# State space layer on one core: layout copies shared by ScalarE and VectorE, two TensorE visits a quarter, gate stores moved in program order

## Chip, core and metric

The kernel runs on one core of a Trainium2 chip. The metric is the device time of one execution in microseconds (us); lower is better. Three executions of the kernel before took 1206.77, 1207.72 and 1211.47 us; their median is 1207.72 us.

## What is computed

The program is one layer of a hybrid backbone: 256 latent tokens and 128 context tokens (384 rows of 2048 channels) go through a modulated norm and one combined input projection, then through two mixers, a bidirectional state space layer (S5) and an attention, whose gated results are projected, merged and projected out. The part that the change touches is the state space layer and the gates next to it:

```python
def _s5_bidir(u, lam_bar, b_bar, c_re, c_im, d, h0_f, h0_b):
    ug = uf.reshape(n, L, SSM_GROUPS, SSM_GROUP).astype(jnp.complex64)
    bu_f = jnp.einsum('blgi,gpi->blgp', ug, b_bar[0])
    bu_b = jnp.einsum('blgi,gpi->blgp', ug, b_bar[1])
    h_f = _lin_scan(bu_f, lam_bar[0], h0_f)
    h_b = jnp.flip(_lin_scan(jnp.flip(bu_b, axis=1), lam_bar[1], h0_b), axis=1)
    y = (einsum('blgp,gip->blgi', h_f, c[0]) + einsum('blgp,gip->blgi', h_b, c[1])).real
...
    ys = ys * jax.nn.sigmoid(ys @ w_glu + b_glu)
    ys = ys * jax.nn.silu(z_s)
    merged = jax.nn.sigmoid(g_s) * p_s + jax.nn.sigmoid(g_a) * p_a
```

There are 64 groups of 16 channels, each with a state of 64 complex numbers, scanned over time in both directions.

## The kernel before

**Big matmuls.** Every projection is done in float32 with each operand split in a high and a low part (`hi`, `lo`; `hh`, `hl` for activations), so a product takes three matmuls. A weight block `raw` of 512 KB is loaded on SP's queue; for each half of it ScalarE writes `hi` (line 70) and VectorE (GpSimd in the first stage) writes `lo` (line 71). One half block is a step: 12 matmuls in `mode_b` (lines 192 to 194) or 9 wider ones in `mode_a` (lines 203 to 205). Four buffers of `raw`, `hi` and `lo` are kept, and `hi` and `lo` are prepared two to three steps ahead.

**Background work.** Everything else is written as Python generators. After the 12 matmuls of a step, `Background.step` lets each generator emit up to its next `yield`; a negative number means "come back so many steps later", a positive one is charged to the step's budget. So the program order of every engine is fixed by steps, and each engine works through its own order and waits at semaphores.

**The state space layer** (`ssm_half`, run twice, for 32 groups each) is such a generator. It has an input phase, a scan and an output phase.

- Input phase: four quarters `e` of 8 groups. `tables` (VectorE, six operations) builds `E`, the input matrices over four time steps; `turn` transposes it on TensorE (line 436) and `turn2` copies the result to `W1` on ScalarE (line 443); `kern` multiplies `CT` by `E` (line 452) and `kern2` picks its blocks to `KS` on VectorE; `drive` multiplies `W1` by the inputs `U` (line 478), once for the real part (`ri` 0) and once for the imaginary part; `drive2` copies each result to `H`, the scan's layout, in four ScalarE copies of 64 partitions by 384 elements (line 489), which write with a stride of 64 elements. `kturn` and `kturn2` transpose `KS` into `Kc`.
- These matmuls use the pool of five PSUM banks `bk`, handed out in rotation. A quarter takes nine: two for `drive` of the imaginary part, one for `kturn`, two for `turn`, two for `kern`, two for `drive` of the real part. So `kern` gets the banks that `drive` of the imaginary part filled five banks earlier.
- TensorE is visited three times in a quarter, a step apart: (`drive` imaginary, `kturn`, `turn`), then (`kern`), then (`drive` real). What drains a visit is emitted one step after it.
- Scan: 64 turns of four small VectorE operations on `H`.
- Output phase: for `x` in 0 to 7, `states` copies the states from `H` into a matmul operand `x4a` or `x4b`, four strided ScalarE copies of 64 by 384 (lines 585, 586); `outs` does 24 small matmuls (lines 597, 600) one step later; `act_out` applies GELU (line 611); `store` writes to DRAM.

**Gates.** `gate_zs` and `gate_gs` (lines 859 to 874) finish eight tiles each of the gates `z_s` and `g_s` right after the first stage and write them to DRAM scratch (`zss`, `gss`, 192 KB a store) through GpSimd's queue, two steps later. They are read again in the second half of the program. They are started from line 925 on, ahead of the state space layer in the list of generators.

In the same stretch SP's queue carries the layer's own inputs (`ssm_read`: C, B, D and the relayout of `U` out of scratch, many rows of 64 to 384 bytes) between the loads of `raw`.

Of the kernel before, what the change touches and what calls it, by code (L numbers as in the profile page):

```python
# [9 lines left out]
AF = mybir.ActivationFunctionType  # L10
# [116 lines left out]
def hybrid(ctx, tc, a):  # L127
    nc = tc.nc
    V, S, PE, GP, SP = nc.vector, nc.scalar, nc.tensor, nc.gpsimd, nc.sync
# [13 lines left out]
    def bank():  # L143
        return psb.tile([128, 512], F32, name="bk")
# [9 lines left out]
    def stt(o, x, s, y, op0, op1):  # L154
        return V.scalar_tensor_tensor(o, x, s, y, op0=op0, op1=op1)
# [232 lines left out]
    def ssm_half(hf, sp, yss):  # L388
        g0 = 32 * hf
        with pool("sh", "right") as t, pool("shx", "right", bufs=1) as tx, pool("shw", "right", bufs=2) as tw:  # L390
# [41 lines left out]
            def turn(e):  # L432
                pb = [bank() for _ in range(2)]
                for ri in range(2):
                    for j in range(4):
                        PE.transpose(pb[ri][:, 128 * j:128 * j + 128],
                                     E[e][:, ri, 2 * j:2 * j + 2].rearrange("p g s i -> p (g s i)"), ident)
                return pb

            def turn2(e, pb):  # L440
                W1[e] = tx.tile([128, 2, 4, 128], F32, name="W")
                for ri in range(2):
                    S.activation(W1[e][:, ri].rearrange("p j q -> p (j q)"), pb[ri], AF.Copy)

            def kern(e):
                pk = [bank() for _ in range(2)]
                for ri in range(2):
                    for j in range(4):
                        for d in range(2):
                            ps_ = slice(64 * d, 64 * d + 64)  # L450
                            gl = slice(8 * e + 2 * j, 8 * e + 2 * j + 2)
                            PE.matmul(pk[d][32 * j:32 * j + 32, 0:128],
                                      CT[ps_, ri, gl].rearrange("p g i -> p (g i)"),
                                      E[e][ps_, ri, 2 * j:2 * j + 2].rearrange("p g s i -> p (g s i)"),
                                      start=ri == 0, stop=ri == 1)
                return pk

            def kern2(e, pk):
                KS[e] = tw.tile([128, 2, 64], F32, name="KS")
                for d in range(2):  # L460
                    ts(KS[e][:, d], pk[d][:, 64:128], sp["ev"][:, 1:2], OP.mult)
                    stt(KS[e][:, d], pk[d][:, 0:64], sp["ev"][:, 0:1], KS[e][:, d], OP.mult, OP.add)

            def kturn(e):
                p = bank()
                for d in range(2):
                    PE.transpose(p[:64, 128 * d:128 * d + 128], KS[e][:, d], ident)
                return p

            def kturn2(e, p):  # L470
                S.activation(Kc[:, :, e], p[:64, 0:256].rearrange("p (d c) -> p d c", d=2), AF.Copy)

            def drive(e, ri):
                pb = [bank() for _ in range(2)]
                for j in range(4):
                    for g2 in range(2):
                        rows = slice(64 * g2, 64 * g2 + 64)
                        PE.matmul(pb[g2][:, 96 * j:96 * j + 96], W1[e][rows, ri, j], U[rows, 4 * e + j],  # L478
                                  start=True, stop=True)
                return pb  # L480

            def drive2(e, ri, pb):
                for g2 in range(2):
                    o = Hs[:, :, 1:33, ri, 8 * e + g2:8 * e + 8:2].rearrange("p b k g -> p g b k")
                    i = pb[g2][:, :384].rearrange("p (g n) -> p g n", g=4)
                    for d in range(2):
                        x = slice(64 * d, 64 * d + 64)
                        i_ = (i[x, :, ::-1] if d else i[x]).rearrange("p g (b k) -> p g b k", b=3)
                        S.activation(o[x], i_, AF.Copy)  # L489

            def ctables():
                for e in range(4):
# [18 lines left out]
            hold = {}  # L511
            for e in range(5):
                while e < 4 and e not in E:
                    yield -1
                if e:
                    drive2(e - 1, 0, hold[0])
                    hold[1] = drive(e - 1, 1)
                    hold["k"] = kturn(e - 1)
                if e < 4:
                    hold["t"] = turn(e)  # L520
                yield -1
                if e:
                    drive2(e - 1, 1, hold[1])
                    kturn2(e - 1, hold["k"])
                if e == 4:
                    break
                turn2(e, hold["t"])
                hold["p"] = kern(e)
                yield -1
                kern2(e, hold["p"])  # L530
                hold[0] = drive(e, 0)
                yield -1

            D2 = t.tile([128, 16, 4, 16], F32, name="x4b")
# [44 lines left out]
            def states(x):  # L579
                HB[x] = t.tile([128, 2, 4, 96], F32, name="x4a" if x % 2 else "x4b")  # L580
                gl = slice(4 * x, 4 * x + 4)
                for ri in range(2):
                    o = HB[x][:, ri].rearrange("p g (b k) -> p g b k", b=3)
                    i = Hs[:, :, 0:32, ri, gl].rearrange("p b k g -> p g b k")
                    S.activation(o[0:64], i[0:64], AF.Copy)
                    S.activation(o[64:128], i[64:128, :, ::-1, ::-1], AF.Copy)

            def outs(x):
                e, h = divmod(x, 2)
# [33 lines left out]
            for x in range(11):  # L623
                while x < 8 and x // 2 not in CL:
                    yield -1
                if x >= 4 and x % 2 == 0:
                    store(x // 2 - 2)
                if 2 <= x < 10:
                    act_out(x - 2)
                if 1 <= x < 9:  # L630
                    outs(x - 1)
                if x < 8:
                    states(x)
                yield -1

    def ssm(sp):
        for hf in range(2):
            yield from ssm_half(hf, sp, yss)
        p = bank()
        fo = ssp.tile([64, 2, 128], F32, name="fo")  # L640
        for ri in range(2):
            PE.transpose(p[:64, 128 * ri:128 * ri + 128], sp["fin"][:, ri], ident)
        S.activation(fo.rearrange("p r c -> p (r c)"), p[:64, :256], AF.Copy)
        for ri, n in enumerate(("out_re", "out_im")):
            SP.dma_start(dram(a[n], 0, [[64, 64], [4096, 2], [1, 64]]), fo[:, ri].rearrange("p (d q) -> p d q", d=2))
        yield 0.1
# [212 lines left out]
    def gate_zs(k):  # L859
        yield -1  # L860
        t = stg.tile([128, TOK], F32, name="sg")
        S.activation(t, zacc[k], AF.Tanh, scale=0.5)
        yield -1
        stt(zacc[k], t, 1.0, zacc[k], OP.add, OP.mult)
        yield -2
        GP.dma_start(zss[k], zacc[k])
        yield 0.1

    def gate_gs(k):
        yield -1  # L870
        S.activation(gacc[k], gacc[k], AF.Tanh, scale=0.5)
        yield -2
        GP.dma_start(gss[k], gacc[k])
        yield 0.1

# [13 lines left out]
    i = 0  # L889
    for s, (k0, nk) in enumerate(slices):  # L890
# [4 lines left out]
        for n in range(2 * len(plan[s])):  # L895
# [12 lines left out]
            for c, pv in enumerate(mode_k(i, hb, uk, kr)):  # L908
                w, k = divmod((c0 % 4096) // 128 + 4 // uk * hb + c, 8)
                if w == 0:  # L910
                    o = ua[:, k].rearrange("p (t n) -> p t n", t=T)
                    pv = pv.rearrange("p (n t) -> p t n", t=T)
                else:
                    o = zacc[k] if w == 1 else gacc[k]
                if kr:
                    tt(o, pv, o, OP.add)
                elif c % 2:
                    V.tensor_copy(o, pv)
                else:
                    S.activation(o, pv, AF.Copy)  # L920
                if end:
                    if w == 0:
                        SP.dma_start(us[k], ua[:, k])
                    elif w == 1:
                        g_zs.append(bg.add(gate_zs(k), True))
                    else:
                        g_zs.append(bg.add(gate_gs(k), True))
# [552 lines left out]
```

## Time and profile before

| | |
|---|---|
| three executions | 1206.77, 1207.72, 1211.47 us |
| the profiled execution | 1211.18 us, span of its core 1209.4 us |
| mean granted clock of TensorE | 0.989 of full speed |
| busy share of the span | TensorE 96%, VectorE 65%, ScalarE 47%, GpSimd 15% |
| HBM | 178 GB/s over the span |

The span runs from the first to the last instruction. The state space layer takes from about 270 to 690 us: its first transposes (`turn`) start at 292.13 and 499.33 us, the scans run from 339.5 to 424 and up to 632 us, and the output phases start at 437.5 and 647.8 us, the second ending at 689 us. An engine that isn't TensorE matters there only where TensorE stands still for it.

### The profile page before, as it was taken

The numbers are of one execution on the slowest core, as the hardware profiler recorded it, in microseconds if no ns is written. First come the engines' busy times: TensorE is split into PE (matmuls) and PEld (weight loads), VectorE is DVE, ScalarE is ACT, GpSimd is POOL, SyncE is SP. The second block draws the span as 40 slices with busy tenths as digits, with TensorE's granted clock in tenths as the row PEclk, the third lists the DMA queues.
The fourth block names the chain that finished last, engine by engine and source line by source line (L and its number), as shares of the span: only waits on it lengthen the run. The fifth ranks groups of instructions, "written<-read, shape, count | busy, mean of one in ns | idle before, by whom it ended". The sixth has DMA issues, their size and how long they took to land.

```text
span 1209.4 us, 19648 instructions
## 1 busy us (share of the span) xinstructions
PE 1159.6 (96%) x7215; PEld 1019.6 (84%) x7215; DVE 784.9 (65%) x1896; ACT 571.3 (47%) x1042; POOL 176.8 (15%) x150
## 2 busy tenths in 40 slices
PE   4899999999999999999999899998999999999997
PEld 3799999998898887989999788876787899878886
DVE  4555555676379963648996434478678846687873
ACT  4343333344853379585337834456454433333332
POOL 2355555672000000000000001110100000000000
PEclk9999999999999999999999999999898999999999
DMA  9987777478255485425544264446454257786661
GB/s 294 327 278 235 248 257 252 120 203 247 78 130 165 146 154 139 142 83 127 170 155 130 77 185 135 130 115 213 149 164 127 88 182 249 258 296 218 215 234 71
DMA packets 216116, 217.38 MB, mean 180 GB/s; under 512 B 64617, under 2 KB 170689, under 8 KB 215636
## 3 DMA queue, kind: packets, MB, share of 16 engines
q1 hardware_dynamic: 213940, 212.73, 58.0%
q0 software_dynamic: 1184, 3.18, 0.9%
q8 instruction: 57, 0.93, 0.3%
q10 hardware_dynamic: 896, 0.21, 0.1%
q14 instruction: 39, 0.32, 0.1%
HBM read 197.90 MB, written 16.87 MB: 178 GB/s over the span
## 4 chain that ended last, share of the span: by engine, by line
PE 78%; ACT 8%; DVE 7%; DMA 3%; issue 3%; SPq 1%; POOL 0%; DVEq 0%; ACTq 0%; POOLq 0%
PE m L192 10%; PE m L194 9%; PE m L193 9%; PE m L203 8%; PE m L205 8%; PE m L204 8%; PE m L854 5%; PE m L856 5%; PE m L855 5%; PE bk L726 2%; DVE lo L71 2%; ACT H L489 1%; PE bk L478 1%; ACT hi L70 1%; PE bk L1025 1%
## 5 line engine op out<-in xcount | busy, mean ns | idle before, releaser
L70 ACT ACTIVATE hi<-raw 128x512 fp32r<-128x512 f32 x464 | 286.9, 629 | 336.4 <-PE m L193 114.1
L71 DVE TENSOR_TENSOR lo<-raw,hi 128x512 fp32r<-128x512 f32 x368 | 250.7, 687 | 220.1 <-ACT hi L70 211.1
L192 PE MATMUL m<-hh,hi 128*128 128x384 f32 x832 | 288.7, 347 | 13.5 <-ACT hi L70 5.0
L194 PE MATMUL m<-hh,lo 128*128 128x384 f32 x832 | 281.2, 338 | 0.2
L193 PE MATMUL m<-hl,hi 128*128 128x384 f32 x832 | 280.5, 337 | 0.0
L203 PE MATMUL m<-hi,hh 128*128 128x512 f32 x480 | 190.4, 397 | 0.0
L205 PE MATMUL m<-hi,hl 128*128 128x512 f32 x480 | 187.5, 391 | 0.0
L204 PE MATMUL m<-lo,hh 128*128 128x512 f32 x480 | 187.3, 390 | 0.0
L192 PEld LDWEIGHTS m<-hh,hi 128*128 128x128 f32 x832 | 157.8, 190 | 28.6 <-ACT hi L70 8.0
L194 PEld LDWEIGHTS m<-hh,lo 128*128 128x128 f32 x832 | 157.7, 190 | 1.4 <-DVE lo L71 1.4
L193 PEld LDWEIGHTS m<-hl,hi 128*128 128x128 f32 x832 | 158.0, 190 | 0.1
L71 POOL TENSOR_TENSOR lo<-raw,hi 128x512 fp32r<-128x512 f32 x96 | 124.8, 1310 | 108.1 <-ACT hi L70 103.8
L854 PE MATMUL m<-hh,hi 128*128 128x384 f32 x384 | 133.1, 346 | 4.6 <-ACT ua L920 1.4
L855 PE MATMUL m<-hl,hi 128*128 128x384 f32 x384 | 129.1, 336 | 0.3 <-POOL hl L147 0.3
L856 PE MATMUL m<-hh,lo 128*128 128x384 f32 x384 | 129.4, 337 | 0.0
L203 PEld LDWEIGHTS m<-hi,hh 128*128 128x128 f32 x480 | 90.4, 188 | 21.4 <-issue 1.4
L205 PEld LDWEIGHTS m<-hi,hl 128*128 128x128 f32 x480 | 90.4, 188 | 19.3
L204 PEld LDWEIGHTS m<-lo,hh 128*128 128x128 f32 x480 | 90.5, 189 | 18.1
L854 PEld LDWEIGHTS m<-hh,hi 128*128 128x128 f32 x384 | 72.6, 189 | 13.5 <-issue 6.2
L855 PEld LDWEIGHTS m<-hl,hi 128*128 128x128 f32 x384 | 72.7, 189 | 0.5 <-POOL hl L147 0.5
L856 PEld LDWEIGHTS m<-hh,lo 128*128 128x128 f32 x384 | 72.5, 189 | 0.0
L147 POOL TENSOR_TENSOR rm<-rn,mhalf 128x24 f32<-128x24 f32 x4 | 18.1, 4515 | 365.2 <-DVE rn L152 365.2
(265 smaller groups left out, 1286.8 us busy)
## 6 DMA issues: line engine op xcount, KB each, us to landing
raw<-in_w_in_dram SPq DMA_DIRECT2D x160, 512.0 KB, 3.8
wa<-in_w_ada_dram SPq DMA_DIRECT2D x32, 1024.0 KB, 7.5
gw<-in_w_ada_dram SPq DMA_DIRECT2D x32, 512.0 KB, 5.8
raw<-in_w_o_dram SPq DMA_DIRECT2D x32, 512.0 KB, 6.1
raw<-in_w_ssm_out_dram SPq DMA_DIRECT2D x16, 512.0 KB, 3.4
raw<-in_w_att_out_dram SPq DMA_DIRECT2D x16, 512.0 KB, 5.8
raw<-in_w_glu_dram SPq DMA_DIRECT2D x8, 512.0 KB, 4.6
tgs<-sg SPq DMA_DIRECT2D x16, 192.0 KB, 1.9
```

Source lines behind the costliest of these rows:

```text
L70: self.nc.scalar.activation(h, t, AF.Copy)
L71: (self.nc.gpsimd if self.low_on_pool else self.nc.vector).tensor_tensor(l, t, f(h), op=OP.subtract)
L192: PE.matmul(o, wh[:, kk, w], xh[q][:, j, :], start=first and hb == 0 and kk == 0, stop=False)
L193: PE.matmul(o, wh[:, kk, w], xl[q][:, j, :], start=False, stop=False)
L194: PE.matmul(o, wl[:, kk, w], xh[q][:, j, :], start=False, stop=last and hb == 1 and kk == 1)
L203: PE.matmul(ps[r], xh[q][:, j, tk], wh, start=first and hb == 0, stop=False)
L204: PE.matmul(ps[r], xh[q][:, j, tk], wl, start=False, stop=False)
L205: PE.matmul(ps[r], xl[q][:, j, tk], wh, start=False, stop=last and hb == 1)
L726: PE.matmul(pab[b][32 * (k % 4):32 * (k % 4) + 32, 0:128 * nk], ct[:, kt, :], wa[s, i][:, k, :], start=kt < 4, stop=kt >= 12)
L854: PE.matmul(o, wh[:, w], hh[q][:, j, :], start=kk == 0, stop=False)
L855: PE.matmul(o, wh[:, w], hl[q][:, j, :], start=False, stop=False)
L856: PE.matmul(o, wl[:, w], hh[q][:, j, :], start=False, stop=kk == nk - 1)
```

## The change

`drive2` gives the bank of the odd groups (`g2` 1) to VectorE and keeps the other on ScalarE. `states` gives the imaginary part (`ri` 1) to VectorE. In the input phase `kern` and `drive` of the real part are emitted together, two steps after `turn`, and their drains `kern2` and `drive2` in the same step, right behind them. The gate stores are emitted 8 + 3k (`z_s`) and 9 + 3k (`g_s`) steps after the gate is done instead of two.

```diff
@@ drive2
                         i_ = (i[x, :, ::-1] if d else i[x]).rearrange("p g (b k) -> p g b k", b=3)
-                        S.activation(o[x], i_, AF.Copy)
+                        if g2:
+                            V.tensor_copy(o[x], i_)
+                        else:
+                            S.activation(o[x], i_, AF.Copy)
@@ the loop over quarters
                 if e:
-                    drive2(e - 1, 0, hold[0])
                     hold[1] = drive(e - 1, 1)
                     hold["k"] = kturn(e - 1)
...
                 turn2(e, hold["t"])
+                yield -1
                 hold["p"] = kern(e)
-                yield -1
+                hold[0] = drive(e, 0)
                 kern2(e, hold["p"])
-                hold[0] = drive(e, 0)
+                drive2(e, 0, hold[0])
                 yield -1
@@ states
-                    S.activation(o[0:64], i[0:64], AF.Copy)
-                    S.activation(o[64:128], i[64:128, :, ::-1, ::-1], AF.Copy)
+                    if ri:
+                        V.tensor_copy(o[0:64], i[0:64])
+                        V.tensor_copy(o[64:128], i[64:128, :, ::-1, ::-1])
+                    else:
+                        S.activation(o[0:64], i[0:64], AF.Copy)
+                        S.activation(o[64:128], i[64:128, :, ::-1, ::-1], AF.Copy)
@@ gate_zs
         stt(zacc[k], t, 1.0, zacc[k], OP.add, OP.mult)
-        yield -2
+        yield -8 - 3 * k
         GP.dma_start(zss[k], zacc[k])
@@ gate_gs
         S.activation(gacc[k], gacc[k], AF.Tanh, scale=0.5)
-        yield -2
+        yield -9 - 3 * k
         GP.dma_start(gss[k], gacc[k])
```

TensorE in the second quarter of the first half, around `kern` (L452). Before:

```order
L193 MATMUL m<-hl_103,hi 128x384
L194 MATMUL m<-hh_99,lo 128x384
L452 MATMUL bk<-E,CT 32x128 x16
L192 MATMUL m<-hh_99,hi 128x384
L193 MATMUL m<-hl_103,hi 128x384
```

And with the change:

```order
L193 MATMUL m<-hl_103,hi 128x384
L194 MATMUL m<-hh_99,lo 128x384
L452 MATMUL bk<-E,CT 32x128 x16
L478 MATMUL bk<-U,W 128x96 x8
L192 MATMUL m<-hh_100,hi 128x384
```

`kern` moved 12 matmuls back, to where `drive` (L478) stood, and 24 matmuls now lie between `turn` and it. In the first quarter of the first half alone `turn` itself also moved, 12 matmuls ahead, because the gates' generators no longer use up the budget of that step.

VectorE in the second half's input phase, from the drain of `kern` (KS) on; `E` and `q` belong to the table of the next quarter. Before:

```order
L155 SCALAR_TENSOR_TENSOR KS<-bk,ev,KS 128x64
L147 TENSOR_TENSOR E<-E,q_5617 128x4x8x16
L147 TENSOR_TENSOR q_5731<-me,preB 128x512
L71 TENSOR_TENSOR lo<-raw,hi 128x512
L147 TENSOR_TENSOR E<-me,preB 128x4x8x16 x2
```

And with the change (`L490` is `drive2`'s copy):

```order
L155 SCALAR_TENSOR_TENSOR KS<-bk,ev,KS 128x64
L490 COPY H<-bk 64x4x3x32 x2
L147 TENSOR_TENSOR E<-E,q_5617 128x4x8x16
L147 TENSOR_TENSOR q_5735<-me,preB 128x512
L71 TENSOR_TENSOR lo<-raw,hi 128x512
L147 TENSOR_TENSOR E<-me,preB 128x4x8x16 x2
L71 TENSOR_TENSOR lo<-raw,hi 128x512
L490 COPY H<-bk 64x4x3x32 x2
```

The last operation of a table now stands behind two copies that wait for `drive`.

GpSimd's queue at the end of the first stage. Before, the first ten of the sixteen stores stand between the last `lo` operations:

```order
L866 DMA zss<-zs_123 128x384
L866 DMA zss<-zs_122 128x384
L71 TENSOR_TENSOR lo<-raw,hi 128x512
L866 DMA zss<-zs_125 128x384
L866 DMA zss<-zs_124 128x384
L71 TENSOR_TENSOR lo<-raw,hi 128x512
L866 DMA zss<-zs_127 128x384
L866 DMA zss<-zs_126 128x384
L71 TENSOR_TENSOR lo<-raw,hi 128x512
L873 DMA gss<-gs_131 128x384
L873 DMA gss<-gs_130 128x384
```

And with the change:

```order
L402 MEMSET DT 128x1024
L873 DMA zss<-zs_122 128x384
L873 DMA zss<-zs_123 128x384
L880 DMA gss<-gs_130 128x384
L880 DMA gss<-gs_131 128x384
L873 DMA zss<-zs_124 128x384
L873 DMA zss<-zs_125 128x384
L880 DMA gss<-gs_132 128x384
L880 DMA gss<-gs_133 128x384
L873 DMA zss<-zs_126 128x384
L873 DMA zss<-zs_127 128x384
L538 MEMSET x4b 128x1024
```

All stores now stand behind the last `lo`, ten of them in one row ahead of the clearing of `x4b` (`D2`, which waits for the last table to have read `B`) and the other six behind it. SP's queue is in the same order before and after.

## Rows read from the trace of the kernel before

**Rows 1.** The page, part 1: busy time, share of the span, instructions.

```profile
PE 1159.6 (96%) x7215; PEld 1019.6 (84%) x7215; DVE 784.9 (65%) x1896; ACT 571.3 (47%) x1042; POOL 176.8 (15%) x150
```

**Rows 2.** Stretches (us): length, busy us (count) of each engine, clock, DMA share, GB/s.

```profile
286.00:290.00 4.00, 1.74 (x5) 1.38 (x6) 1.73 (x3) 1.64 (x3) 0.00 (x0) 0.80 1.07 317
...
345.00:425.00 80.00, 80.00 (x382) 69.67 (x381) 76.94 (x293) 27.60 (x47) 0.00 (x0) 1.00 0.57 153
...
450.00:460.00 10.00, 7.24 (x55) 6.01 (x54) 2.76 (x5) 9.81 (x17) 0.00 (x0) 1.00 1.01 156
...
640.00:700.00 60.00, 56.50 (x413) 48.06 (x412) 28.60 (x54) 46.82 (x72) 0.00 (x0) 0.97 0.35 100
```

**Rows 3.** The timeline of TensorE: start us, us, operation, [idle before, releaser].

```profile
281.12 0.33 PE L192 MATMUL m<-hh,hi 128*128 128x384 f32 x1
...
283.20 0.33 PE L192 MATMUL m<-hh,hi 128*128 128x384 f32 x1
...
295.18 0.67 PE L452 MATMUL bk<-E,CT 64*32 64x128 f32 x32
295.78 0.44 PE L192 MATMUL m<-hh,hi 128*128 128x384 f32 x1
...
305.83 0.40 PE L452 MATMUL bk<-E,CT 64*32 64x128 f32 x2
...
307.45 0.45 PE L192 MATMUL m<-hh,hi 128*128 128x384 f32 x1
...
309.76 1.14 PE L478 MATMUL bk<-U,W 64*128 64x96 f32 x16
```

**Rows 4.** Who waited for whom, whole span: us in total, times, longest.

```profile
PEld bk L452 <- ACT H L489: 6.1, 7, 1.4
```

**Rows 5.** Groups of instructions: line, engine, operation, tiles, count, busy us, mean ns.

```profile
L71 DVE TENSOR_TENSOR lo<-raw,hi 128x512 fp32r<-128x512 f32 x368 | 250.7, 687 | 220.1 <-ACT hi L70 211.1
...
L489 ACT ACTIVATE H<-bk 64x384 f32<-64x384 f32 x64 | 54.1, 845 | 15.4 <-PE bk L478 14.5
...
L1068 DVE COPY PT<-bk 128x384 f32<-128x384 f32 x16 | 8.1, 549 | 0.0
...
L147 DVE TENSOR_TENSOR hl<-sg,hh 128x384 fp32r<-128x384 f32 x8 | 6.5, 850 | 2.2 <-ACT hh L1302 1.9
...
L155 DVE SCALAR_TENSOR_TENSOR KS<-bk,ev,KS 128x64 f32<-128x64 f32 x16 | 4.5, 284 | 0.6
```

**Rows 6.** The timeline of ScalarE in the first output phase, one period of `x`.

```profile
464.01 0.68 ACT L611 ACTIVATE yg<-bk 64x192 f32<-64x192 f32 x2 [0.18 <-PE bk L600]
...
468.94 0.66 ACT L611 ACTIVATE yg<-bk 64x192 f32<-64x192 f32 x2
```

**Rows 7.** The timeline of TensorE in the first output phase: a wait and two visits.

```profile
456.92 0.44 PE L192 MATMUL m<-hh,hi 128*128 128x384 f32 x1 [2.60 <-ACT sg L1199]
...
466.19 0.55 PE L597 MATMUL bk<-x4b,W 128*64 128x96 f32 x8
...
470.07 0.55 PE L597 MATMUL bk<-x4a,W 128*64 128x96 f32 x8
```

**Rows 8.** The chain that ended last, around 280 us: start us, us, what.

```profile
279.80 7.67 DMA raw<-in_w_in_dram
```

**Rows 9.** The timeline of TensorE and VectorE behind that load.

```profile
288.26 0.55 PE L192 MATMUL m<-hh,hi 128*128 128x384 f32 x1 [2.30 <-ACT hi L70]
...
289.57 0.69 DVE L147 TENSOR_TENSOR E<-E,q 128x512 f32<-128x512 f32 x1
...
292.13 1.03 PE L436 MATMUL bk<-ident,E 128*128 128x128 f32 x8
```

**Rows 10.** DMA queues from 264 to 288 us: packets, MB, share of 16 engines.

```profile
q0 software_dynamic: 1024, 3.15, 37.6%
```

**Rows 11.** The timeline of GpSimd: its last `lo`, and what follows its stores.

```profile
270.90 1.30 POOL L71 TENSOR_TENSOR lo<-raw,hi 128x512 fp32r<-128x512 f32 x1
...
314.23 0.95 POOL L535 MEMSET x4b<- 128x1024 f32 x1 [33.75 <-DVE q L147]
```

## The prediction, made before the changed kernel was run

> **What bounds the kernel now.** I first looked at the busy shares on the page: TensorE is busy for 1159.6 of 1209.4 us [rows 1], so only its 50 us of idle time, and what it does at a lower clock, can be won. Next I read the stretches [rows 2], to see in which of them it stands still: not in a scan (80.00 of 80 us busy, with VectorE at 76.94), but next to the scans, in the input and output phases and where the first of them begins. Third, the timeline of TensorE there [rows 3] and the waits [rows 4], to see whom it waits for: ScalarE's copies to and from `H` in both phases, and one weight load at 288 us.
>
> **Input phase.** A step of 12 matmuls takes 2.08 us unbroken (281.12 to 283.20) but 2.31 us from the end of one visit to the start of the next (307.45 to 309.76), so a visit costs 0.23 us beside its own matmuls [rows 3]. `kern` takes 0.60 us where it does not wait (295.18 to 295.78), and 1.62 us in the second quarter (305.83 to 307.45) [rows 3]: two of its matmuls go, then it waits for the bank that `drive2` is still emptying. Over the program its weight loads wait 6.1 us for those copies [rows 4]; six quarters have the wait, the first of each half has not.
>
> With the change `kern` stands two steps after `turn` and its banks' drain is two copies on each of two engines instead of four in a row on one. Two ScalarE copies of 0.845 us [rows 5] and `hi`, `Kc` and `W1` behind them are over well before 24 matmuls (4.2 us) are. So the 6.1 us go. The eight visits that fall away, one in each quarter, give 8 x 0.23 = 1.8 us. **Term B: -7.9 us.**
>
> What is late next is VectorE. Its new copy, 64 partitions by 384 elements from PSUM, written with a stride, is not in the trace. Below it lies a copy of 384 contiguous elements from PSUM, 0.549 us; above it an operation of 384 elements that reads with a long stride, 0.850 us [rows 5]. ScalarE takes 0.845 us for the same strided copy, so I take 0.85 and keep 0.55. In a quarter VectorE then has three `lo` and six table operations of the same size (9 x 0.69), four for `KS` (4 x 0.284) and four copies (4 x 0.85): 10.7 us [rows 5], if nothing overlaps. TensorE's quarter is 11.7 us now (three steps of 2.31, `kern` 1.62, the rest visits), and would be 10.4. The two are level, and only while a table is being built, beside three of a half's four quarters. The drains now wait at the head of VectorE's queue for TensorE to reach `drive`, and behind them stand the next table's last operation and `lo`. `lo` is two steps ahead, so 4.6 us of cover; the table's last operation ends 2 x 0.85 + 0.7 us = 2.4 us after `drive`, and `turn` wants it one step, `drive` and `kturn` later, some 3.6 us after. It fits with 1.2 us to spare, which a copy of 1.45 us would use up. I charge nothing for it.
>
> **Output phase.** One `x` takes ScalarE 4.93 us (464.01 to 468.94) [rows 6] and TensorE 3.88 us (466.19 to 470.07) [rows 7]. ScalarE falls back by 1 us with each `x` until the two steps of cover are gone; then TensorE waits: 2.60 us at 456.92 [rows 7], and 3.5 us between 640 and 700 us, where it is busy for 56.50 of 60 us [rows 2]. There the clock is at 0.97 on the mean [rows 2]: TensorE, after standing still, runs a part of the stretch at the lower (1.2 GHz) of its levels, and over 60 us that is worth 1.8 us. Two of the four copies gone, ScalarE needs 4.93 - 2 x 0.85 = 3.2 us an `x` and is faster than TensorE; VectorE needs 2 x 0.85 + 0.69 = 2.4 us, 3.8 with two table operations, just below 3.88. So the waits go: 2.6 + 3.5 + 1.8 = 7.9 us. I leave 0.4 for the first `x` of a half, where tables and copies meet. **Term C: -7.5 us.**
>
> The clock's 1.8 us hang on the idle time. But after 2.60 us of idle time ahead of 456.92 [rows 7] the clock of that stretch stayed at 1.00 [rows 2]. The Trainium skill, "TensorE: Matmul & The Clock Gate", section "What's actually happening", says that the slow clock is the default and that activity releases it; by this rule the 1.8 us come back with the waits. By the row at 456.92 alone the two are not tied, and the sum would be 1.8 us smaller.
>
> **The start of the first half.** A `raw` load issued at 279.80 lands 7.67 us later, at 287.5 [rows 8]. TensorE waits 2.30 us for it and then takes 3.87 us for 12 matmuls (288.26 to 292.13) [rows 9] instead of 2.31: 1.56 us, since the clock is at 0.80 there, partly at 1.2 GHz [rows 2]. That is 3.9 us to win. In this stretch the 16 engines are full (DMA share 1.07) [rows 2], and the gate stores on GpSimd's queue use 37.6% of 24 us, 9.0 us for 16 stores or 0.56 us each [rows 10]. But a later place in program order does not by itself hold a store back: GpSimd's last `lo` ends at 272.2 us [rows 11], and after it nothing but the clearing of `DT` stands ahead of ten of the stores, so these go one behind the other from some 273 us on, while the load is under way. Only the six behind the clearing of `x4b`, which waits until 314 us [rows 11], leave the crowded stretch. That moves 6 x 0.56 = 3.4 us of transfers away, so the load lands between 284.1 (all of it gained) and 287.5 us (nothing gained).
>
> Against it stands that `turn` of the first quarter has moved ahead of these 12 matmuls. It needs the last operation of the first table, which stands on VectorE behind the `lo` of this very load and ends at 290.26, 2.8 us after it landed [rows 8, 9]. TensorE would reach `turn` at 285.96 (288.26 less the wait) and stand until landing + 2.8: 0.9 us with a landing at 284.1, 4.3 us at 287.5. So the place changes by -3.0 us (0.9 for 2.3, and the clock back) to +2.0 us. I take the middle. **Term A: -0.5 us.** The moved drains, the six late stores and the swapped copies add no instruction to TensorE, and SP's queue keeps its order; the late stores meet DMA engines that are mostly idle.
>
> **Sum.** -7.9 - 7.5 - 0.5 = -15.9 us. The profiled execution took 1211.18 us, which gives 1195.3; it lies 3.5 us above the median of the three, 1207.72, from which I get 1191.8. I forecast 1192 us.
>
> **The rivals.**
>
> R1, the gates are not spread. Of the sixteen stores ten still leave together, right when the load is on its way; then it lands at 287.5 as before, and the early `turn` makes the place worse. For it speaks the order of GpSimd's queue; against it that none goes before 273 us any more. Term A is +2.0 instead of -0.5: 1194.5, say 1195 us. The Trainium skill, "DMA: Bandwidth & Descriptors", section "Queues, rings and completion order", says that each DMA engine takes turns between the queues that have work, packet by packet; by this rule the load's delay follows from what is outstanding beside it and not from what went before, which is this rival. No row here shows single packets.
>
> R2, VectorE takes ScalarE's place in the input phase: at 1.1 us or more a copy its quarter (9 x 0.69 + 4 x 0.284 + 4 x 1.1 = 11.7 us) is as long as today's, and only the merged visits of term B are left: 1192 + 6.1 = 1198 us. For it speaks that the two engines are level at 0.85 already; against it that the longest row of 384 elements is 0.85 us [rows 5] and that each half's last quarter has no table beside it.
>
> R3, what is won before a scan is lost in it: VectorE is busy for 76.94 of 80 us there [rows 2]. If it enters with a backlog of more than 3.1 us, TensorE waits for `lo` in the scan and term B is gone in both halves: 1192 + 7.9 = 1200 us. Against it: the last quarters have no tables, so the backlog has gone by then.
>
> R4, slower. The in-order wait: `lo` stands behind `kern2` and the two copies, which wait for `drive`. It decides once two copies, the table's last operation and `lo` (2 x copy + 2 x 0.69) take longer than the 4.6 us of cover, so from 1.6 us a copy. At 2.0 us VectorE's quarter is 9 x 0.69 + 4 x 0.284 + 4 x 2.0 = 15.3 us against 11.7 now. Over the six quarters with tables that is +22 us; the output phase (2 x 2.0 + 0.69 = 4.7 us an `x`, near ScalarE's 4.93 now) wins nothing: 1207.7 + 22 = 1230 us. Only the strided write speaks for it; the row of ScalarE's same write, 0.845 us [rows 5], speaks against.
>
> **How the numbers follow.** A measurement of this kernel can tell about 0.5%, 6 us, from no change. The forecast has 0.65, R1 0.13, R2 0.11, R3 0.08, R4 0.03. The forecast's own range is 1185 to 1197: below, all 3.9 us of the load and 0.55 us copies, and some 3 us in which the profiled execution may have stood still more than the median; above, the clock's 1.8 us not coming back and half a microsecond a quarter of late tables. R2 and R3 end at 1198 and 1200, so the range is 1184 to 1200. Faster by over 0.5% means below 1201.7: the forecast, R1, R2 and 0.02 of R3, which ends close to that bound, 0.91. The rest of R3 is within 0.5%: 0.06. Slower: 0.03.
>
> **What would show it.** Right: `kern` in 0.60 us with `drive` right behind it and no wait for `H`; VectorE's copies at 0.55 to 0.85 us; ScalarE below 85% in the output phases, TensorE without the waits at their ends; ten stores in one row from 273 us on, six behind the clearing of `x4b`. Wrong: copies above 1.1 us; TensorE idle before `turn` for more than 2 us at 286 (term A); new waits of TensorE for `lo` or for a table.

## The result and the profile after

The changed kernel takes **1192.12 us** (median of 4 runs, 1188.56 to 1198.52) where the kernel before takes 1209.3 us on the same chip. The ratio is **0.9852**, 95% interval 0.9825 to 0.988: faster by 1.2 to 1.75%. In a later set of runs the same kernel came to 0.9877 (0.9857 to 0.9898), so single sets differ by some 3 us. The forecast was 1192.0 us. Its sum held; of its three terms one, the output phase, was 4 us too small, beyond its interval. One of `split_only`'s eight executions took 2892.59 us and is left out of its ratio.

The page of the changed kernel, part 1: busy time, share of the span, instructions.

```profile
PE 1144.7 (96%) x7215; PEld 1011.2 (85%) x7215; DVE 834.2 (70%) x1960; ACT 519.6 (44%) x978; POOL 176.3 (15%) x150
```

Against [rows 1], 64 instructions and 52 us left ScalarE, and 49 us came to VectorE. TensorE keeps its 7215 matmuls and yet is busy for 15 us less. The stretches say why (length, busy us of each engine, clock, DMA share, GB/s), here of the changed kernel:

```profile
286.00:290.00 4.00, 2.77 (x17) 2.77 (x18) 3.93 (x7) 2.13 (x4) 0.00 (x0) 1.00 0.62 191
300.00:340.00 40.00, 40.00 (x392) 37.24 (x391) 33.29 (x65) 25.32 (x39) 4.09 (x7) 1.00 0.40 125
345.00:425.00 80.00, 80.00 (x375) 68.75 (x374) 76.76 (x280) 27.54 (x46) 0.00 (x0) 1.00 0.56 153
425.00:461.00 36.00, 36.00 (x278) 32.14 (x278) 26.63 (x44) 25.89 (x41) 0.00 (x0) 1.00 0.87 172
640.00:700.00 60.00, 60.00 (x423) 49.43 (x422) 31.99 (x60) 32.31 (x60) 0.00 (x0) 1.00 0.47 136
```

In 640 to 700 us TensorE was busy for 56.50 of 60 us at a clock of 0.97, and ScalarE for 46.82 [rows 2]; now TensorE has no gap, its clock is at 1.00 and ScalarE needs 32.31 (the output phase lies some 12 us earlier here; from 628 to 688 us TensorE has no gap either, and ScalarE is busy for 34.81). The scan (345 to 425) is as it was. The timeline of TensorE shows the rest (start us, us, operation, [idle before, releaser]); the changed kernel in the first half's input phase:

```profile
296.40 0.44 PE L192 MATMUL m<-hh,hi 128*128 128x384 f32 x1 [1.38 <-ACT sg L1202]
...
306.22 0.67 PE L452 MATMUL bk<-E,CT 64*32 64x128 f32 x32
306.82 1.14 PE L478 MATMUL bk<-U,W 64*128 64x96 f32 x16
```

`kern` goes through in 0.60 us with `drive` right behind it, in every quarter; the 6.1 us of [rows 4] are gone. But TensorE has a new wait at 296.40, which no step of the prediction had.

To compare stages without the shift between the traces, the table takes when single visits start, from the view of their lines: the first `turn` (L436), the last `drive` (L478) of the first half and so on. Lengths in us, from each event to the next; "out" is the product with `DT` in `outs`.

| from ... to | before | `gates_only` | `in_only` | `out_only` | after |
|---|---|---|---|---|---|
| start of the program ... first `turn` | 292.1 | 285.5 | 293.1 | 291.2 | 285.4 |
| ... last `drive`, first half | 45.7 | 51.5 | 41.3 | 45.7 | 46.6 |
| ... first out (the scan) | 105.9 | 105.9 | 105.9 | 106.0 | 105.9 |
| ... last out, first half | 35.7 | 37.1 | 37.3 | 32.2 | 32.2 |
| ... first `drive`, second half | 25.9 | 25.9 | 25.6 | 25.8 | 25.6 |
| ... last `drive`, second half | 39.1 | 39.1 | 36.9 | 39.1 | 36.9 |
| ... first out (the scan) | 109.6 | 109.3 | 109.3 | 109.4 | 109.3 |
| ... last out, second half | 34.5 | 34.7 | 34.6 | 29.9 | 29.9 |
| ... end | 520.9 | 518.3 | 518.0 | 518.3 | 515.0 |

The middle columns are the first experiments. The first two rows have to be taken together, since the spread gates pull the first `turn` 12 matmuls ahead. Ahead of every other event stand equally many big matmuls in all five. The last row has nothing of the change in it and still differs by up to 6 us; most of that is the clock. Stretches of the kernel before and of the changed kernel:

```profile
800.00:940.00 140.00, 129.61 (x722) 106.11 (x720) 111.61 (x294) 69.74 (x175) 10.75 (x3) 0.95 0.51 158
800.00:940.00 140.00, 129.01 (x770) 108.82 (x769) 112.47 (x299) 72.83 (x184) 6.29 (x2) 1.00 0.49 156
```

0.95 over 140 us is worth 7 us; the three columns between have 0.98. The traces of the two outer columns are of executions of 1211.18 us, 3.5 above the median before, and of 1188.56 us, 3.6 below the median after, so they lie further apart than the medians do.

### The profile page after: what moved, and what is told of

It is laid out like the page before. It is cut to its first block, busy times and chain, and to the rows that moved or that the text cites. A ratio compares the mean times of both kernels' runs of the same rounds, so it can differ in the third digit from the quotient of the medians.

```text
span 1186.8 us, 19637 instructions
## 1 busy us (share of the span) xinstructions
PE 1144.7 (96%) x7215; PEld 1011.2 (85%) x7215; DVE 834.2 (70%) x1960; ACT 519.6 (44%) x978; POOL 176.3 (15%) x150
## 4 chain that ended last, share of the span: by engine, by line
PE 87%; DVE 5%; ACT 3%; DMA 2%; issue 2%; SPq 1%; POOL 0%; ACTq 0%; DVEq 0%; POOLq 0%
PE m L192 11%; PE m L194 11%; PE m L193 11%; PE m L203 9%; PE m L204 9%; PE m L205 9%; PE m L861 6%; PE m L862 5%; PE m L863 5%; PE bk L733 2%; PE bk L478 1%; PE bk L604 1%; PE bk L607 1%; PE bk L1032 1%; DMA raw<-in_w_in_dram 1%
```

## The experiments

Changes in us below are the ratio's distance from 1 times the median of before in the same set (1211.06, 1210.09, 1209.62 us).

**Each part alone.** Three kernels are the one before with one part of the diff, and a fourth is the changed kernel without the spread gates (yields -2 again).

`gates_only`:

```diff
-        yield -2
+        yield -8 - 3 * k
         GP.dma_start(zss[k], zacc[k])
...
-        yield -2
+        yield -9 - 3 * k
         GP.dma_start(gss[k], gacc[k])
```

> The kernel before with the gate stores spread and nothing else. The theory (term A): the raw load of the first half is issued some 4 us earlier and lands at 284 instead of 287.5, but the turn visit is pulled ahead of its table and waits, so 0 to 4 us are won, about 2; the clock in 286 to 294 is 1.00 instead of about 0.8. Rival R1 (the queue shares bandwidth whatever the order of the stores): nothing, ratio 1.000 within 0.002, and the raw load still lands about 287.5.

> The changed kernel with the gate stores back at their old places. The theory: loses what the spread brought, 0 to 4 us against the changed kernel (ratio to before 0.985 to 0.989), and PE again runs at a low clock between 286 and 294. R1: same as the changed kernel, 0.985.

Measured: 0.9993 (0.9977 to 1.0009), -0.8 us, and `gates_back` 0.9858 (0.9839 to 0.9877), no different from the changed kernel. The spread gates are worth nothing that can be measured. The load that the prediction has landing at 287.5 shows it. ScalarE takes up its two halves when it has landed; in the changed kernel, and in the same kernel run again:

```profile
284.49 1.16 ACT L70 ACTIVATE hi<-raw 128x512 fp32r<-128x512 f32 x2 [6.72 <-DMA raw<-in_w_in_dram]
```

```profile
288.21 1.15 ACT L70 ACTIVATE hi<-raw 128x512 fp32r<-128x512 f32 x2 [7.63 <-DMA raw<-in_w_in_dram]
```

In the six traces without the spread it lies between 283.97 and 288.68 us, in the eight with it between 284.00 and 288.21: run against run differs more than kernel against kernel. The low clock was no sign either: 270 to 300 us have it at 0.94 in `gates_only` and `gates_back`, and at 1.00 in `in_only`, which has no spread.

`in_only` is the diff's `drive2` and its loop over quarters; `out_only` is its `states`.

> The kernel before with the input phase alone changed (copies of drive shared, two visits a quarter). The theory (term B): -7.9 us, ratio 0.9935, no wait of the kern visit for a copy to H. R2 (VectorE takes ScalarE's place): about -4, ratio 0.997, and waits of PE for VectorE in 300 to 340.

Measured: 0.9947 (0.9927 to 0.9966), -6.4 us (-8.8 to -4.1). In the table the first two rows, up to the first half's last `drive`, lose 3.4 us, and the second half's input phase (rows 5 and 6) 2.5.

> The kernel before with the states' imaginary parts copied by VectorE and nothing else. The theory (term C): -7.5 us, ratio 0.994, PE without gaps in 440 to 460 and in 640 to 700, clock 1.00 there. R3 (won time lost elsewhere): under 3 us, ratio 0.998 or above.

Measured: 0.9903 (0.9887 to 0.9919), -11.8 us (-13.7 to -9.8), clearly more than either theory. The table finds 4.6 us of it in the second half and 3.5 in the first against before's own trace, 4.9 to 5.1 in the first against `gates_only` and `in_only`, which have the same output phase as before. What differs is the clock. Before's trace keeps 1.00 after the 2.60 us wait [rows 7]; `in_only` has the same wait, then this (stretches as above, and the row of the wait ahead of them):

```profile
453.56 0.44 PE L192 MATMUL m<-hh,hi 128*128 128x384 f32 x1 [2.58 <-ACT sg L1202]
```

```profile
425.00:461.00 36.00, 33.26 (x223) 29.82 (x222) 19.98 (x32) 30.42 (x44) 0.00 (x0) 0.95 0.82 160
450.00:454.00 4.00, 1.42 (x8) 1.09 (x7) 0.00 (x0) 3.92 (x7) 0.00 (x0) 1.00 0.95 178
454.00:458.00 4.00, 4.00 (x16) 4.00 (x15) 3.42 (x6) 3.94 (x8) 0.00 (x0) 0.57 0.44 119
```

16 matmuls in 4 us at 0.57: most of it ran at 1.2 GHz, which cost (1 - 0.57) x 4 = 1.7 us. Of five traces with this wait three show the drop (`gates_only`, `in_only`, `order_only`; 0.95 in each over the phase) and two don't (before, `split_only`). With the change there is no wait and no drop. `out_only`, the same stretches:

```profile
425.00:461.00 36.00, 36.00 (x257) 32.30 (x256) 30.41 (x50) 23.61 (x38) 0.00 (x0) 1.00 0.87 177
640.00:700.00 60.00, 60.00 (x432) 50.73 (x431) 37.25 (x69) 35.35 (x61) 0.00 (x0) 1.00 0.41 115
```

The parts add up: -0.8 - 6.4 - 11.8 = -19.0 us, against -17.9 (0.9852) for all of them.

**The order or the sharing?** I had given `kern`'s vanished wait to both. `order_only` is before with the visits merged and every copy on ScalarE; `split_only` is before with `drive2`'s copies shared and the old order.

```diff
@@ order_only: the loop over quarters
                 if e:
-                    drive2(e - 1, 0, hold[0])
                     hold[1] = drive(e - 1, 1)
...
                 turn2(e, hold["t"])
+                yield -1
                 hold["p"] = kern(e)
-                yield -1
+                hold[0] = drive(e, 0)
                 kern2(e, hold["p"])
-                hold[0] = drive(e, 0)
+                drive2(e, 0, hold[0])
                 yield -1
@@ split_only: drive2
-                        S.activation(o[x], i_, AF.Copy)
+                        if g2:
+                            V.tensor_copy(o[x], i_)
+                        else:
+                            S.activation(o[x], i_, AF.Copy)
```

> The kernel before with the input phase's two visits a quarter and all copies left on ScalarE. Theory: it was the place of kern that removed its wait, so most of the input phase's gain comes from the order alone, -4 to -5 us (0.996), but ScalarE's four copies at the head of its queue (4 x 0.85 = 3.4 us) delay the evacuations of PSUM behind them by 1.7 us more than in the changed kernel, so each half keeps a wait of 2.5 to 3 us. Rival: the sharing of the copies is what counts, and the order alone brings nothing or loses (1.000 or above).

> The kernel before with drive2's copies shared and the visits in the old order. Theory: two copies in a row (1.7 to 2.1 us) instead of four (3.4 us) empty the bank before kern wants it, so the 6.1 us of kern's waits go without the order too; the drains stand a step later than in the changed kernel, so no PSUM evacuation is held up: -6 us (0.995), as good as both together. Rival: the order is needed, kern still waits 0.5 us or more in each of six quarters: -3 us or less (0.9975 or above).

Measured: `order_only` 0.9981 (0.9967 to 0.9996), -2.3 us; `split_only` 0.994 (0.9918 to 0.9962), -7.3 us, as good as both together. Either of the two takes `kern`'s wait away: in neither trace does it wait for a copy to `H` any more. `split_only` in the second quarter, `kern` in its old place (TensorE, start us, us):

```profile
306.90 0.67 PE L452 MATMUL bk<-E,CT 64*32 64x128 f32 x32
307.50 0.44 PE L192 MATMUL m<-hh,hi 128*128 128x384 f32 x1
```

But only the sharing brings the whole gain. With the order alone TensorE then waits for an evacuation behind ScalarE's four copies. The waits of TensorE in the second half's input phase, 484 to 546 us (waiting line, released by: us, times, longest), of `order_only`, and a stretch right behind this wait:

```profile
PE m L192 <- ACT sg L1199: 2.7, 1, 2.7
```

```profile
530.00:534.00 4.00, 4.00 (x25) 3.36 (x24) 1.22 (x2) 1.09 (x2) 0.00 (x0) 0.50 0.91 283
```

The wait costs the clock as well. The granted clocks on record say the same of all executions: 0.9885 on the mean of 10 of `order_only`, 0.9907 of 19 of before, over their spans some 2.6 us more lost to the lower clock. By this estimate the order by itself is worth the 4 to 5 us that I expected, and the clock takes back about half. The order with the drains a step later and all copies on ScalarE was not run; whether it would do as well as the sharing is open.

The waits of the changed kernel, the first half (284 to 336 us) and then the second:

```profile
PE m L192 <- ACT sg L1202: 1.4, 1, 1.4
PE bk L436 <- DVE E L147: 1.3, 1, 1.3
```

```profile
PE m L192 <- ACT sg L1206: 1.0, 1, 1.0
```

`split_only` has no wait of TensorE at all there, and its second input phase is the shorter one, 36.2 us against 36.9.

**The new wait.** Where it comes from can be read on ScalarE's timeline of the changed kernel:

```profile
293.78 2.06 ACT L492 ACTIVATE H<-bk 64x384 f32<-64x384 f32 x2 [3.95 <-PE bk L478]
295.85 0.87 ACT L1202 ACTIVATE sg<-m 128x384 f32<-128x384 f32 x2
```

ScalarE stood for 3.95 us in front of two copies that wait for `drive`, and `sg`, which empties a bank of the gates that TensorE wants at 295.02, stood behind them. Emitting the drains a step later puts them behind `sg`:

```diff
                 hold["p"] = kern(e)
                 hold[0] = drive(e, 0)
+                yield -1
                 kern2(e, hold["p"])
                 drive2(e, 0, hold[0])
-                yield -1
```

> The changed kernel with kern2 and drive2 of the real part emitted one step later, just ahead of drive of the imaginary part. Theory: TensorE's new waits for the evacuation of the gates' bank (1.38 us in the first half, 1.00 in the second) come from the copies to H waiting at the head of ScalarE's queue; they go, -2.4 us against the changed kernel (ratio to before 0.983). Rival: the waits move to kturn, which follows at once on the drains and needs KS: no gain or a loss (0.985 or above).

Measured: 0.9838 (0.9814 to 0.9863). Both waits for `sg` are gone from the trace (one wait of 1.0 us for the first table is all that is left in the input phases), and the second half's input phase falls from 36.9 to 35.6 us. The size fits -2.4 us, but the ratio alone could not tell it from the changed kernel.

**The early `turn`.** The changed kernel once more, and with the first `turn` put back a step:

```diff
+                if e == 0 and hf == 0:
+                    yield -1
                 if e < 4:
                     hold["t"] = turn(e)
```

> The changed kernel once more, as the level for the other runs of this set: ratio to before 0.985, within 0.983 to 0.988.

> The changed kernel with the first quarter's turn put back one step (12 matmuls), where it stood before; the gate stores stay spread. Theory (term A's second half): its wait for the table (1.3 us in the changed kernel, 1.0 and 2.1 in two others) goes and nothing replaces it, -1 to -2 us against the changed kernel (0.9835 to 0.984). Rival: the wait is only another form of the late raw load, and the 12 matmuls then wait for it: same as the changed kernel, 0.985.

> The changed kernel with three edits together: drains one step later, VectorE's backward copies first, the first turn a step later. Theory: TensorE has none of the three waits left (1.3 + 1.4 + 1.0 us), -3 to -4 us against the changed kernel, 0.982. Rival: what is won in the input phase is taken up elsewhere, 0.985.

Measured: `after_again` 0.9877 (0.9857 to 0.9898), `turn_later` 0.9836 (0.9814 to 0.9857), `best` 0.9833 (0.9811 to 0.9855). In `after_again` the load landed late, and the early `turn` paid for it:

```profile
290.95 1.12 PE L436 MATMUL bk<-ident,E 128*128 128x128 f32 x4 [4.38 <-DVE E L147]
```

Over the six traces with the early `turn` this wait is 0.69 to 4.38 us. In `turn_later` 12 matmuls wait instead, 2.9 us for the load, so the wait changes its place as the rival said; but the shifted step also takes the first half's `sg` wait away. By their ratios `turn_later` and `best` are some 5 us faster than the changed kernel in this set, and some 2 us faster than in its first set: a gain by the set that has all three, of a size that these runs don't fix. `best` is no faster than `turn_later` alone; in its trace a wait of 2.2 us for the load is left.

**Rival R2 and R4's arithmetic.** All of `drive2` on VectorE (`if g2` becomes `if True`):

> The changed kernel with all of drive2's copies on VectorE. By the budget of a quarter: VectorE is free for 10.45 - 8.5 = 2 us a quarter and gets four more copies of 0.85, so it needs 11.9 us (operations of the table and of lo follow at 0.60) against TensorE's 10.45: +1.5 us a quarter in the six quarters with tables, +9 us against the changed kernel (0.992). If VectorE's copies waiting at its queue's head hold up lo and the tables as rival R4 has it, more: +20 us (1.002). If the copies slow each other only when two engines write, and nothing waits, no change (0.985).

Measured: 0.9957 (0.9942 to 0.9971), 0.0080 or 9.7 us more than `after_again` on the same chip; the budget said 9. The quarters do not share it evenly, as the budget had it: from `turn` to `turn` those of the second half take 10.42, 11.99 and 13.69 us, against 10.41, 10.45 and 11.72 in `after_again`. TensorE now waits for VectorE, at 284 to 340 us (first fence) and 484 to 546 us:

```profile
PE bk L436 <- DVE H L490: 3.0, 4, 1.0
PE bk L436 <- DVE E L147: 0.7, 1, 0.7
PE bk L478 <- DVE KS L155: 0.2, 1, 0.2
```

```profile
PE bk L436 <- DVE E L147: 3.5, 2, 1.7
PE bk L436 <- DVE H L490: 1.2, 2, 0.6
```

So the limit that R2 and R4 had in mind is there, at twice the copies.

**Do the two engines slow each other?** `crossed` lets VectorE take the backward direction (partitions 64 to 127) first, ScalarE the forward one:

```diff
-                    for d in range(2):
+                    for d in ((1, 0) if g2 else (0, 1)):
```

> The changed kernel with VectorE copying the backward direction first, so that the two engines write different partitions of H at the same time. If the slowing of a simultaneous pair (1.03 us each, 0.85 each when apart) comes from writing the same partitions, the pairs fall back to 0.85 on each engine; if it comes from the two engines being active at once on PSUM and SBUF, they stay at 1.03. The time is the same in both cases within 1 us (0.985): no one waits for these copies.

Measured: 0.9862 (0.9839 to 0.9885), as expected; what it showed stands in the last section.

## Why the prediction came out right

- **What bounds the kernel, right.** TensorE's gaps, and its clock behind them, were the matter; the scans are the same in all columns of the table to 0.3 us, so R3 (won time lost in a scan) is out.
- **Term B, mechanism half right, -7.9 forecast, -6.4 (-8.8 to -4.1) measured.** `kern`'s 6.1 us went. The merged visits were sized about right: the second half's first quarter, which has no wait, went from 10.62 us (before, 499.33 to 509.95) to 10.41 (after, 489.98 to 500.39), 0.21 for the visit instead of 0.23, so 1.7 us for eight. The step that failed is "I charge nothing for it": I had looked for what waits behind the drains on VectorE's queue, and there nothing did. It was ScalarE's queue, where `sg` stood behind the other two copies: 1.38 us in the first half (none in `in_only`, where the first `turn` is a step later) and 1.00 in the second. For `in_only` 6.1 + 1.7 - 1.0 gives 6.8 us. The interval holds the forecast too.
- **Its cause, one too many.** I gave the vanished wait to the place of `kern` and to the two copies together. Either does it alone (`order_only`, `split_only`), and the place by itself brings a wait of its own.
- **Term C, mechanism right, -7.5 forecast, -11.8 (-13.7 to -9.8) measured.** The waits were sized right; the term that was too small is the clock, 1.8 us of the sum. I counted its cost in the second half and, from one trace, none at 456.92. Three of five traces do pay there. The table accounts for 8.1 to 9.8 us. The granted clocks on record with every execution place the rest: 0.9901 on the mean of 17 of before and 0.9944 of 5 of `out_only`, over their spans of 1209 and 1197 us 12.0 and 6.7 us lost. By this estimate the clock brought 5.3 of the 11.8 us, and the 6.5 that are left are close to the 6.1 of the two waits. Where these executions lost it is not shown, since a trace was kept of one of each.
- **The clock paragraph.** "By the row at 456.92 alone the two are not tied" was read from a lucky execution: the same wait lowers the clock in three traces and not in two. The Trainium skill, "TensorE: Matmul & The Clock Gate", section "What's actually happening", had it that activity releases a slow default, and that the moment of its release varies between runs of one kernel. The traces agree with the first (0.57 in 454 to 458 us of `in_only`, right behind the wait). The second they do not show; what varies in them is whether the clock falls at all: from 425 to 461 us it is 0.95 in `in_only` and 1.00 in `split_only`, which have the same code there.
- **Term A, too small to be told from nothing, -0.5 forecast, -0.8 (-2.8 to +1.1) measured.** "-3.0 to +2.0" came from a landing anywhere between 284.1 and 287.5 and a stall of 0.9 to 4.3 us before `turn`; the traces have 284.0 to 288.2 and 0.69 to 4.38. R1 was as good a description: the load lands no earlier for the spread, over all traces. GpSimd's timeline is as forecast, ten stores between the clearings and six behind the second:

```profile
271.94 0.96 POOL L402 MEMSET DT<- 128x1024 f32 x1
272.83 1.10 POOL L873 DMA_DIRECT2D zss<-zs  x2
...
279.07 1.07 POOL L873 DMA_DIRECT2D zss<-zs  x2 [1.95 <-DMA zss<-zs]
316.43 0.95 POOL L538 MEMSET x4b<- 128x1024 f32 x1 [36.28 <-DVE q L147]
317.32 1.07 POOL L880 DMA_DIRECT2D gss<-gs  x2
```

- **R2 and R4, wrong as expected.** They needed copies of 1.1 and 1.6 us on VectorE; the mean is 0.920, a little above the 0.85 that I took. The groups of the changed kernel (operation, count, busy us, mean ns, then the idle time before it), with ScalarE's 845 of [rows 5] to compare:

```profile
L492 ACT ACTIVATE H<-bk 64x384 f32<-64x384 f32 x32 | 29.8, 932 | 32.8 <-PE bk L478 32.3
L490 DVE COPY H<-bk 64x384 f32<-64x384 f32 x32 | 29.4, 920 | 0.7 <-PE bk L478 0.3
...
L592 ACT ACTIVATE x4b<-H 64x384 f32<-64x384 f32 x8 | 7.2, 904 | 0.1
...
L590 DVE COPY x4b<-H 64x384 f32<-64x384 f32 x8 | 5.0, 623 | 0.1
```

So the match to 0.1 us is luck. Term C was too small by 4 us, and what was measured for term B is 1.5 us less than forecast. The forecast takes 15.9 us off 1207.72 us; by the ratio 17.9 came off, and the kernel before took 1209.3 us in the set of the result. The median itself moves by 2 to 3 us from set to set.

## What to carry to other kernels

When work moves to an earlier place in an in-order queue, list what stands behind it on every queue that it is on, the one that it leaves half of as well. A wait that one trace shows to be free of a clock penalty may cost one in the next execution: count idle time of TensorE with the clock drop unless several traces deny it. And a shared copy can bring all that a reordering seems to bring, so change the two apart.

## What the runs showed of the hardware

Two engines that copy on the same partitions slow each other, but only when they start almost together. In the changed kernel both take the forward direction first, and where they start together both get slower, 1.06 us a copy; where VectorE starts 0.7 us, nearly a copy, later, each takes 0.85. A third of a microsecond apart, with the larger part of each copy still side by side on the same partitions, it is 0.88 already (last line of each). ScalarE's and VectorE's timelines, two copies a line:

```profile
300.91 1.71 ACT L492 ACTIVATE H<-bk 64x384 f32<-64x384 f32 x2 [2.63 <-PE bk L478]
307.98 2.13 ACT L492 ACTIVATE H<-bk 64x384 f32<-64x384 f32 x2 [3.48 <-PE bk L478]
...
318.43 1.77 ACT L492 ACTIVATE H<-bk 64x384 f32<-64x384 f32 x2 [3.45 <-PE bk L478]
```

```profile
301.61 1.70 DVE L490 COPY H<-bk 64x384 f32<-64x384 f32 x2
308.03 2.12 DVE L490 COPY H<-bk 64x384 f32<-64x384 f32 x2
...
318.76 1.75 DVE L490 COPY H<-bk 64x384 f32<-64x384 f32 x2
```

`crossed`, where they have different partitions when they start together, turns it round: the pair that starts together is fast, and the one 0.7 us apart, whose second and first copy now meet on the same partitions, is slower:

```profile
301.97 1.85 ACT L492 ACTIVATE H<-bk 64x384 f32<-64x384 f32 x2 [2.63 <-PE bk L478]
309.04 1.73 ACT L492 ACTIVATE H<-bk 64x384 f32<-64x384 f32 x2 [3.33 <-PE bk L478]
```

```profile
302.67 1.84 DVE L490 COPY H<-bk 64x384 f32<-64x384 f32 x2
309.18 1.69 DVE L490 COPY H<-bk 64x384 f32<-64x384 f32 x2
```

Over the nine traces with shared copies it is a matter of the distance between the two starts. On the same partitions a copy takes on the mean 1.05 us where they start within 0.05 us (77 pairs), 0.97 at 0.12 to 0.20 us (11 pairs), 0.91 at 0.20 to 0.30 (17 pairs) and 0.85 at 0.30 to 0.45 (27 pairs). On different partitions, started within 0.15 us of each other, copies take 0.79 to 0.88 us. So it is not the partitions alone, nor the two engines being busy at once; why a short lead is enough was not found.

The Trainium skill, "SBUF — State Buffer", section "SBUF: two separate sides", says that ScalarE and VectorE's own ports never wait on anyone. The copies write `H` in SBUF, and they also read two banks of PSUM in the same partitions; whether the reading or the writing costs the 0.2 us was not told apart. If it is the writing, these rows don't agree with that sentence, and the measurement decides. A copy of the same size from SBUF to SBUF, `states`', which reads with the long stride and writes in a row, takes VectorE 0.60 to 0.62 us and ScalarE 0.88 to 0.90.
